# A hybrid attention layer: the first weight tiles are loaded directly behind the value slices, and the bias rows are read later

## The chip, the core and the metric

The kernel runs on one core of a Trainium2 chip. The metric is the device time of one execution in microseconds, the median of several runs. The core has five engines that run side by side and meet at semaphores: TensorE (matrix products, PE in the profile), ScalarE (ACT), VectorE (DVE), GpSimd (POOL) and SyncE (SP), which here issues nearly all transfers between the main memory and the on-chip memory.

## The reference, cut to what matters

```python
h = x @ W_in                                   # x: 256 x 1024, split into the parts below
ya = swa_sink_attention(qa, ka, va, sinks, table_a) * silu(za)   # window 128, 8 heads, 2 key heads
yb = moba_attention(qb, kb, vb, table_b) * silu(zb)              # 256 tokens: one causal block
merged = sigmoid(ga + b) * (ya @ w_out_a) + sigmoid(gb + b) * (yb @ w_out_b)
x = layer_norm(alpha * x + merged @ w_out, gamma, beta)
```

There are 256 tokens, 8 heads of width 64 in each of the two branches, and everything is float32. Both attentions add a learned bias to the scores that depends on the distance of query and key only.

## The kernel before, in words

**Products in three parts.** Each float32 matrix is split into a high part (a rounded copy) and a low part (what is left), and a product is high × high + low × high + high × low. In `contract` (L181, L182, L184) the two products with the high weights come first for all eight slices of the contraction, and then eight with the low weights. A weight tile therefore needs three steps before it is used up to its end: a load into a raw buffer (L133 on SP), a cast to the high part on ACT (L138), and a subtraction for the low part on DVE (L153).

**The stages.** First come the value projections: eight slices ("v", 0 to 7), each with its slice of x. Then 37 tiles ("t", n) of 512 KB, each one projection of 128 columns: t0 holds the keys of the first branch, t1 to t4 its queries, t5 to t12 keys and queries of the second branch in turn, t13 to t20 the inner gates, t21 to t36 the outer gates. The output weights ("a", "b", "o") follow.

**The order of the work is written out by hand.** Each engine executes its instructions in the order in which the program emits them. The list `order` (L93 to L105) says in which order things are fetched, with the bias rows ("r", n) placed between the tiles. `lead` (L167) is called just before a tile is used. It moves two cursors along `order`: the first calls `fetch` (the load, and the cast on ACT), the second calls `split` (the subtraction on DVE) and stays one item behind. How far ahead of the tile in use the cursors go is `far`, counted without the bias rows: 2 for the value slices, 2 for t0 to t2, 3 for t3 to t20, and so on. There are five raw buffers (`RAWS`), so a load has to wait for the split of the fifth item before it, and eight buffers each for high and low parts.

**What stands between.** `keys` (L192) and `queries` (L202) project a tile and take the result out of the accumulator with ACT and DVE: L196, L198 and a copy on POOL (L200) for the keys, L208 and L210 for the first queries (t1), L215, L216 and POOL copies (L220, L221) for the others. `scores` (L224) multiplies queries and keys, adds the bias rows `toep` (L235, L248), and takes the exponential on ACT (L250). `normalise` (L261) divides by the sums (L263 to L273), `turn` (L275) transposes on TensorE (L281).

The loop from L346 runs twelve steps. For the first steps it emits: step 0, the projection of t1; step 1, that of t2 and the first `scores`; step 2, `normalise` of those first scores, then the lead and the projection of t3, and the second `scores`; step 3, the projection of t4, the transposes of the first scores, and the third `scores`. At the head of each step stands `lead`, so that the casts and splits which it emits come ahead of the evictions of that step in the queues of ACT and DVE.

**The bias rows.** Each ("r", n) issues two transfers of 128 KB in pieces of 1 KB (L120). They read a small buffer in main memory that the kernel itself has written (L325), and the scores number n read them.

Of the kernel before, what the change touches and what calls it, by code (L numbers as in the profile page):

```python
# [35 lines left out]
KA, QA, KQB, ZA, ZB, GA, GB = 0, 1, 5, 13, 17, 21, 29  # L36
# [10 lines left out]
def hybrid_layer(ctx: ExitStack, tc: tile.TileContext, xT, x2, w_t, w_v, w_a, w_b, w_o,  # L47
# [43 lines left out]
    xh = const.tile([P, NK, S], F32R, name="xh")  # L91
    xl = const.tile([P, NK, S], F32R, name="xl")
    order = [("v", k) for k in range(NK)]  # L93
    for t in range(GA):
        order += [("t", t)]
        if QA <= t < KQB:
            order.append(("r", t - QA))
        elif KQB < t < ZA and (t - KQB) % 2:
            order.append(("r", 4 + (t - KQB) // 2))
    for g, w in ((GA, "a"), (GB, "b")):  # L100
        for c in range(8):
            order.append(("t", g + c))
# [3 lines left out]
    ahead = {"v": 2, "t": 3, "a": 4, "b": 5, "o": 7}  # L106
# [51 lines left out]
    def advance(stage, at, far):  # L158
        at += 1
        while at < len(order) and far:  # L160
            far -= order[at][0] != "r"
            at += 1
        while cursors[stage] < at:
            (fetch, split)[stage](*order[cursors[stage]])
            cursors[stage] += 1

    def lead(kind, n):  # L167
        at = order.index((kind, n))
        far = ahead[kind] if kind != "t" else 2 if n < 3 else 3 if n < GA else 4 if n < GB else 5
        advance(0, at, far)  # L170
        advance(1, at, far - 1)

    def weights(kind, n):
        lead(kind, n)
        return ready[kind, n]
# [170 lines left out]
    for i in range(12):  # L346
        if i == 2:
            normalise(*raised[0], True)
        lead("t", QA + i if i < 4 else KQB + 2 * (i - 4) if i < 8 else ZA + i - 8)
        if 3 <= i < 10:  # L350
            normalise(*raised[i - 2], i == 9)
        if 4 <= i < 8:
            keys(KQB + 2 * (i - 4), 1 + i % 2)
        if i < 8:
            queued[i] = queries(QA + i if i < 4 else KQB + 2 * (i - 4) + 1)
        else:
            acc = project(ZA + i - 8)
        if i >= 5 and i % 2:
            attend([(turned[n], 0 if n < 4 else P + (n - 4) * P) for n in (i - 5, i - 4)], ov[:, i - 5:i - 3, :])
        if 3 <= i < 11:  # L360
            turned[i - 3] = turn(raised[i - 3][0])
        if 1 <= i < 9:
            n = i - 1
            raised[n] = scores(queued[n], 0 if n < 4 else 1 + n % 2, 2 * n, 2 * n if n < 4 else None)
        if i >= 8:
            gate(i - 8, acc)
# [190 lines left out]
```

## Time and profile before

| | |
|---|---|
| median of three runs | 198.87 us (198.54 to 199.08) |
| the profiled execution | 198.86 us |
| its span on the core | 197.1 us |
| TensorE busy | 188.0 us (95%) |
| DVE, ACT, POOL busy | 136.7, 112.5, 44.1 us |
| moved by transfers | 37.43 MB, mean 190 GB/s |

The span is the time from the first to the last recorded instruction; the execution's own time holds some 1.8 us more. A row of the timeline gives the start in us, the duration in us, the engine, the line of the kernel, the operation, what it writes and reads, and in brackets the idle time of the engine before it with what ended it. Neighbouring instructions of one kind are merged ("x2").

### The profile page before, as it was taken

The page shows a single profiled execution, that of the slowest core. Times are in us where ns is not written, and L with a number is a line of the kernel's source. Part 1 is how long each engine was busy: PE and PEld are TensorE (multiplying, and loading weights), DVE is VectorE, ACT ScalarE, POOL GpSimd, SP SyncE. Part 2 cuts the span into 40 slices and gives each one's busy share as a digit, 9 for nine tenths or more (in the row PEclk, how much of TensorE's full clock was granted, in tenths as well). Part 3 has the DMA queues.
Part 4 walks back from the last instruction along what each step waited for, and adds up shares of the span by engine and source line. Part 5 has one row for each costly group of instructions (what it writes and reads, how often), then busy time and mean ns, then how long its engine had stood idle before and what let it go on. Part 6 is the DMA issues. An engine that isn't in the chain of part 4 may idle for free.

```text
span 197.1 us, 3919 instructions
## 1 busy us (share of the span) xinstructions
PE 188.0 (95%) x1469; PEld 178.0 (90%) x1469; DVE 136.7 (69%) x280; ACT 112.5 (57%) x223; POOL 44.1 (22%) x89
## 2 busy tenths in 40 slices
PE   8999999699999999999999999999999999999970
PEld 3799999599999999989999999999999999888860
DVE  0596277987897796686777547447585878696873
ACT  5575757479679669766679444246554746540110
POOL 7020043456599683100000000000000000004230
PEclk9999999999999999999999999999999999999996
DMA  5999999774363454044667865474847499400202
GB/s 139 306 400 346 266 288 318 193 249 149 120 195 126 122 147 166 7 150 170 209 209 234 299 221 152 170 224 145 288 145 266 139 323 334 170 0 0 104 3 106
DMA packets 14082, 37.43 MB, mean 190 GB/s; under 512 B 1632, under 2 KB 5744, under 8 KB 14064
## 3 DMA queue, kind: packets, MB, share of 16 engines
q1 hardware_dynamic: 13520, 36.51, 57.4%
q0 software_dynamic: 256, 0.49, 0.7%
q8 instruction: 11, 0.18, 0.4%
q10 hardware_dynamic: 288, 0.20, 0.3%
q14 instruction: 7, 0.06, 0.1%
HBM read 35.75 MB, written 1.44 MB: 189 GB/s over the span
## 4 chain that ended last, share of the span: by engine, by line
PE 77%; DMA 13%; DVE 4%; SPq 1%; issue 1%; ACT 1%; DVEq 0%; ACTq 0%
PE ps_acc L181 19%; PE ps_acc L182 19%; PE ps_acc L184 19%; PE ps_acc L424 6%; DMA wraw<-in_w_v 5%; DMA wraw<-in_w_t 5%; PE ps_sc L424 4%; DMA toep<-rd 4%; PE ps_pt L281 3%; PE ps_o L300 2%; DVE wl L153 2%; PE ps_sc L241 2%; PE ps_pt L424 1%; PE ps_sc L233 1%; PE ps_o L302 1%
## 5 line engine op out<-in xcount | busy, mean ns | idle before, releaser
L181 PE MATMUL ps_acc<-xh,wh 128*128 128x256 f32 x296 | 71.7, 281 | 0.0
L182 PE MATMUL ps_acc<-xl,wh 128*128 128x256 f32 x296 | 71.4, 280 | 0.0
L153 DVE TENSOR_TENSOR wl<-wraw,wh 128x1024 fp32r<-128x1024 f32 (+1 forms) x53 | 61.2, 1170 | 5.4 <-ACT wh L138 4.3
L138 ACT ACTIVATE wh<-wraw 128x1024 fp32r<-128x1024 f32 (+2 forms) x54 | 52.7, 989 | 8.4 <-DMA wraw<-in_w_t 5.0
L181 PEld LDWEIGHTS ps_acc<-xh,wh 128*128 128x128 f32 x296 | 55.8, 189 | 0.2 <-issue 0.2
L182 PEld LDWEIGHTS ps_acc<-xl,wh 128*128 128x128 f32 x296 | 55.8, 188 | 0.0
L184 PE MATMUL ps_acc<-xh,wl 128*128 128x256 f32 x296 | 41.0, 281 | 0.7 <-DVE wl L153 0.7
L184 PEld LDWEIGHTS ps_acc<-xh,wl 128*128 128x128 f32 x296 | 37.5, 188 | 0.9 <-DVE wl L153 0.9
L412 POOL CAST wh<-sums 128x2 fp32r<-128x2 f32 x8 | 1.5, 182 | 93.7 <-ACT sums L408 93.7
L379 ACT ACTIVATE sg<-ps_acc,bg 128x256 f32<-128x256 f32 x16 | 7.6, 475 | 19.3 <-PE ps_acc L184 19.2
L181 PE MATMUL ps_acc<-yh,wh 128*128 128x256 f32 x64 | 15.8, 281 | 0.0
L182 PE MATMUL ps_acc<-yl,wh 128*128 128x256 f32 x64 | 15.8, 280 | 0.0
L200 POOL CAST kall<-kall 64x512 fp32r<-64x512 f32 x10 | 10.7, 1065 | 14.9 <-DVE kall L198 14.3
L384 DVE TENSOR_TENSOR ga<-ps_acc,sg 128x256 f32<-128x256 f32 x8 | 3.4, 424 | 13.9 <-ACT wh L138 13.9
L181 PEld LDWEIGHTS ps_acc<-yh,wh 128*128 128x128 f32 x64 | 12.1, 188 | 0.0
L182 PEld LDWEIGHTS ps_acc<-yl,wh 128*128 128x128 f32 x64 | 12.0, 188 | 0.0
L389 ACT ACTIVATE mm<-m 128x256 fp32r<-128x256 f32 x8 | 3.4, 419 | 12.0 <-DVE m L388 12.0
L184 PE MATMUL ps_acc<-yh,wl 128*128 128x256 f32 x64 | 10.1, 279 | 0.0
L150 DVE TENSOR_TENSOR wl<-wraw,wh 128x1024 fp32r<-128x1024 f32 x8 | 9.7, 1218 | 0.1
L198 DVE TENSOR_TENSOR kall<-ps_acc,kall 64x256 fp32r<-64x256 f32 x10 | 4.2, 423 | 7.6 <-ACT kall L196 7.5
L424 PE MATMUL ps_acc<-wh,mm 128*128 128x512 f32 x32 | 8.8, 396 | 0.0
L184 PEld LDWEIGHTS ps_acc<-yh,wl 128*128 128x128 f32 x64 | 8.6, 188 | 0.0
(177 smaller groups left out, 302.6 us busy)
## 6 DMA issues: line engine op xcount, KB each, us to landing
wraw<-in_w_t SPq DMA_DIRECT2D x37, 512.0 KB, 3.9
wraw<-in_w_o SPq DMA_DIRECT2D x8, 512.0 KB, 5.0
wraw<-in_w_v SPq DMA_DIRECT2D x7, 320.0 KB, 5.3
toep<-rd SPq DMA_DIRECT2D x16, 128.0 KB, 7.0
wraw<-in_w_a SPq DMA_DIRECT2D x4, 512.0 KB, 3.3
wraw<-in_w_b SPq DMA_DIRECT2D x4, 512.0 KB, 4.5
xraw<-in_xT SPq DMA_DIRECT2D x8, 128.0 KB, 5.1
xr<-in_x SPq DMA_DIRECT2D x1, 1024.0 KB, 8.0
```

The source lines that it names most:

```text
L138: nc.scalar.activation(wh[:, cut], raw[:, cut], AF.Copy)
L150: nc.vector.tensor_sub(quarters(wl), raw.rearrange("p (a b) -> p a b", a=4), quarters(wh).bitcast(F32))
L153: nc.vector.tensor_sub(wl[:, :width], raw[:, :width], wh[:, :width].bitcast(F32))
L181: nc.tensor.matmul(acc, wh[:, cols[k]], ah[:, a0 + k, :], start=(k == 0), stop=False)
L182: nc.tensor.matmul(acc, wh[:, cols[k]], al[:, a0 + k, :], start=False, stop=False)
L184: nc.tensor.matmul(acc, wl[:, cols[k]], ah[:, a0 + k, :], start=False, stop=(k == n - 1))
L198: nc.vector.tensor_sub(l[r, j, :], acc[r, :], h[r, j, :].bitcast(F32))
L200: nc.gpsimd.tensor_copy(kall[halves[1 - j], b, :, j, :], kall[r, b, :, j, :])
L241: nc.tensor.matmul(o[:, j, :], q[:, j, P:], kall[:, b, part, j, :], start=(j == 0 and part == 0), stop=(j == 1 and part == 1))
L281: nc.tensor.transpose(pt[:, b * P:(b + 1) * P], pr[:, j, b * P:(b + 1) * P], ident)
L379: nc.scalar.activation(sg, acc, AF.Sigmoid, bias=bg[:, at:at + 1])
L424: nc.tensor.matmul(acc, a[:, k, ts], w[:, q:q + n, :cols], start=s0, stop=s1)
```

## The change

The bias rows leave their places behind t1, t2, t3, t4, t6, t8, t10, t12 and come behind t3 (two pairs), t4, t5, t7, t9, t11 and t13. `far` is 4 for all tiles up to t28 (it was 2 for t0 to t2 and 3 for t3 to t20). For the value slices, `far` grows at the end: `max(2, n - 3)` gives 3 for slice 6 and 4 for slice 7. In the order of emission this gives:

| at the lead of | fetched before | split before | fetched after | split after |
|---|---|---|---|---|
| v6 | t0 | v7 | t0 t1 | v7 t0 |
| v7 | t1 | t0 | t2 t3 | t1 t2 |
| t0 | r0 t2 | t1 | r0 r1 t4 | t3 |
| t1 | r1 t3 | t2 | r2 t5 | t4 |
| t2 | r2 t4 | t3 | r3 t6 | t5 |
| t3 | r3 t5 t6 | t4 t5 | t7 | t6 |
| t4 | r4 t7 | t6 | r4 t8 | t7 |
| t5 | t8 | t7 | t9 | t8 |

From there on everything is fetched and split one tile further ahead than before until t20, and from t22 on both orders are the same. No computation is added or removed.

```diff
     order = [("v", k) for k in range(NK)]
+
+    rows_at = {3: (0, 1), 4: (2,), 5: (3,), 7: (4,), 9: (5,), 11: (6,), 13: (7,)}
     for t in range(GA):
-        order += [("t", t)]
-        if QA <= t < KQB:
-            order.append(("r", t - QA))
-        elif KQB < t < ZA and (t - KQB) % 2:
-            order.append(("r", 4 + (t - KQB) // 2))
+        order += [("t", t)] + [("r", n) for n in rows_at.get(t, ())]
...
     def lead(kind, n):
         at = order.index((kind, n))
-        far = ahead[kind] if kind != "t" else 2 if n < 3 else 3 if n < GA else 4 if n < GB else 5
+        far = ahead[kind] if kind != "t" else 4 if n < GB else 5
+        if kind == "v":
+
+            far = max(far, n - 3)
         advance(0, at, far)
         advance(1, at, far - 1)
```

## The prediction

> **What bounds the kernel now.** I read the slices of the page first, then TensorE's own rows around the one bad slice, then what ACT, DVE and the loads did before it. Below, t0, t1, … are weight tiles in the order of use; r0, r1, … are pairs of bias rows, two transfers each; T4, T5, T6 are the times at which t4, t5, t6 have landed; "scores 0" is the first call of `scores`.
>
> ```profile
> PE   8999999699999999999999999999999999999970
> ```
>
> A slice is 4.93 us. TensorE is full from the second slice to the tail, except in the eighth (34.5 to 39.4 us). A tile that is ready earlier anywhere else buys nothing, and a delay that TensorE takes here is carried to the end, since no later slice has room.
>
> ```profile
> 29.15 0.40 PE L233 MATMUL ps_sc<-kall,q 128*128 128x256 f32 x2
> ...
> 29.87 0.28 PE L181 MATMUL ps_acc<-xh,wh 128*128 128x256 f32 x1
> ...
> 32.69 0.40 PE L233 MATMUL ps_sc<-kall,q 128*128 128x256 f32 x2
> ...
> 33.40 0.28 PE L181 MATMUL ps_acc<-xh,wh 128*128 128x256 f32 x1
> ...
> 35.17 0.28 PE L182 MATMUL ps_acc<-xl,wh 128*128 128x256 f32 x1
> 36.19 1.21 PE L184 MATMUL ps_acc<-xh,wl 128*128 128x256 f32 x8 [0.74 <-DVE wl L153]
> 37.23 0.82 PE L281 MATMUL ps_pt<-ident,pr__426 128*128 128x128 f32 x6
> 38.95 0.74 PE L233 MATMUL ps_sc<-kall,q 128*128 128x256 f32 x2 [0.90 <-DVE nm L248]
> ...
> 40.24 0.28 PE L181 MATMUL ps_acc<-xh,wh 128*128 128x256 f32 x1
> ```
>
> Scores 0 starts at 29.15 and takes 0.72; t3 takes 29.87 to 32.69 (2.82); scores 1 takes 0.71; t4 starts at 33.40. t4 then stops for the low part of its weights until 36.19, scores 2 waits until 38.95, and t5 starts at 40.24. The transposes in between take this long where nothing is waited for (chain of waits):
>
> ```profile
> 46.09 0.66 PE ps_pt L281 x6
> ```
>
> Without stops t5 would start at 33.40 + 2.82 + 0.66 + 0.71 = 37.6. The whole prize is 2.6 us. Who is late is seen on DVE:
>
> ```profile
> 27.76 0.88 DVE L210 SCALAR_TENSOR_TENSOR q<-ps_acc,q 64x256 fp32r<-64x256 f32 x2 [0.83 <-ACT q L208]
> 28.67 1.23 DVE L153 TENSOR_TENSOR wl<-wraw,wh 128x1024 fp32r<-128x1024 f32 x1
> 30.32 0.42 DVE L216 SCALAR_TENSOR_TENSOR ql<-ps_acc,qh 128x256 fp32r<-128x256 f32 x1 [0.42 <-ACT qh L215]
> ...
> 33.62 0.16 DVE L263 TENSOR_TENSOR sm<-sm,es 128x4 f32<-128x4 f32 x1 [0.75 <-ACT es L258]
> ...
> 34.03 0.97 DVE L270 TENSOR_SCALAR pr__426<-pr__426,rs 128x256 f32<-128x256 f32 x2
> 34.92 2.55 DVE L153 TENSOR_TENSOR wl<-wraw,wh 128x1024 fp32r<-128x1024 f32 x2
> 37.39 0.41 DVE L216 SCALAR_TENSOR_TENSOR ql<-ps_acc,qh 128x256 fp32r<-128x256 f32 x1
> ```
>
> This is one chain: L216 of t2 (30.32), the softmax of scores 0, its normalisation (33.62 to 35.0), the splits of t4 and t5 (2.55), L216 of t3 (37.39), and 2.85 later t5 on TensorE. The split of t4 stands behind the normalisation by program order alone, and so stops TensorE at 35.17.
>
> **The change part by part.** ACT's rows show its queue: each cast L138 of a tile stands where its load is issued, ahead of the evictions of that step.
>
> ```profile
> 17.30 1.06 ACT L138 ACTIVATE wh<-wraw 128x1024 fp32r<-128x1024 f32 x1 [0.62 <-DMA wraw<-in_w_t]
> 19.30 1.06 ACT L138 ACTIVATE wh<-wraw 128x1024 fp32r<-128x1024 f32 x1 [0.94 <-DMA wraw<-in_w_t]
> ...
> 22.93 1.06 ACT L138 ACTIVATE wh<-wraw 128x1024 fp32r<-128x1024 f32 x1 [1.10 <-DMA wraw<-in_w_t]
> 23.89 0.76 ACT L196 ACTIVATE kall<-ps_acc 64x256 fp32r<-64x256 f32 x2
> 25.86 1.07 ACT L138 ACTIVATE wh<-wraw 128x1024 fp32r<-128x1024 f32 x1 [1.22 <-DMA wraw<-in_w_t]
> 26.96 0.77 ACT L208 ACTIVATE q<-ps_acc 64x256 fp32r<-64x256 f32 x2
> 28.81 1.06 ACT L138 ACTIVATE wh<-wraw 128x1024 fp32r<-128x1024 f32 x1 [1.08 <-DMA wraw<-in_w_t]
> 29.90 0.39 ACT L215 ACTIVATE qh<-ps_acc 128x256 fp32r<-128x256 f32 x1
> ```
>
> The casts of t0 to t4 each wait for the load; t2, t3, t4 stand ahead of L196, L208, L215, the evictions of t0, t1, t2. With the change, `lead` asks for four tiles ahead where it asked for two, so the casts ahead of these three evictions are those of t4, t5 and t6. The splits on DVE move up with them: t4 ahead of L210, t5 ahead of L216 of t2, and only t6 behind the normalisation.
>
> *The split that leaves the chain.* Between normalisation and L216 of t3 stands one split of 1.23, not two of 2.55: 1.3 us gained. The stop of t4 at 35.17 goes with it.
>
> *The casts that come early.* Everything now hangs on T5 and T6. The chain of waits has the load of t6 (start, duration), and windows show the pace of the loads (time; last two columns: DMA share, GB/s):
>
> ```profile
> 24.11 8.92 DMA wraw<-in_w_t
> ```
> ```profile
> 14.00:17.00 3.00, 3.00 (x23) 3.00 (x22) 2.06 (x5) 1.79 (x3) 0.00 (x0) 1.00 1.03 414
> ...
> 20.00:23.00 3.00, 3.00 (x26) 3.00 (x25) 1.23 (x1) 1.86 (x6) 0.00 (x0) 1.00 1.06 270
> 23.00:26.00 3.00, 3.00 (x28) 3.00 (x27) 1.26 (x3) 1.77 (x4) 0.69 (x2) 1.00 1.06 267
> ...
> 48.50:49.50 1.00, 1.00 (x11) 1.00 (x10) 0.97 (x2) 0.44 (x2) 1.00 (x1) 1.00 0.85 267
> ```
>
> Before, t6 landed at 33.0. The loads are saturated: share over 1. At 414 GB/s, with no bias rows, a tile of 512 KB takes 1.27. A tile with a pair of rows takes 2.94 (22.93 to 25.86 to 28.81), which is the 267 to 270 GB/s of these windows. Rows alone, from the last window, take 0.84 a pair (256 KB at 267/0.85). So a mixture of rows and tiles costs some 0.8 more than both apart, a loss that the new order meets less often. From t0 at 17.3: t1, t2, t3 without rows at 1.27 each, 21.1; then r0, r1 and t4, 2.94 + 0.84 to 1.47 (half of 2.94), T4 = 24.9 to 25.5; r2 and t5, 2.94, T5 = 27.8 to 28.4; r3 and t6, 2.94, T6 = 30.8 to 31.4. But the bytes ahead of t6 are the same as before, t0 to t5 and four pairs, so if the loss goes by bytes, T6 stays 33.0 and T5 is r3's 0.84 to 1.5 ahead of where it was. I take T6 = 31.6, nearer to the grouped sum, and T5 = 28.6; the ends are 30.8 and 33.0. Issue does not hold this back:
>
> ```profile
> 13.44 0.82 DVE L153 TENSOR_TENSOR wl<-wraw,wh 128x640 fp32r<-128x640 f32 x1
> ...
> 15.17 0.83 DVE L153 TENSOR_TENSOR wl<-wraw,wh 128x640 fp32r<-128x640 f32 x1 [0.57 <-ACT wh L138]
> ```
> ```profile
> 14.32 1.26 SPq L120 DMA_DIRECT2D toep<-rd  x2
> 15.67 0.54 SPq L133 DMA_DIRECT2D wraw<-in_w_t  x1
> 16.26 1.16 SPq L120 DMA_DIRECT2D toep<-rd  x2
> 17.52 0.53 SPq L133 DMA_DIRECT2D wraw<-in_w_t  x1
> ```
>
> SP is passed in order, and five raw buffers mean that t2 needs the split of value slice 5 (ends 14.26) and t3 that of slice 6 (16.00). So t2's issue moves only from 15.67 to 14.3 and t3's from 17.52 to 16.0, still 5 us ahead of their landing; r0 and r1 (four issues of about 0.6) follow by 18.5.
>
> *TensorE at scores 0.* It needs the query of t1: cast of t5 (T5 + 1.06), then L208 to the end of L210, 26.96 to 28.64 = 1.68: T5 + 2.75 = 31.35, where it was 29.15, a stop of 2.2 us. The keys of t0 (L196 at T4 + 1.06, then copies on POOL) end earlier:
>
> ```profile
> 25.25 2.16 POOL L200 CAST kall<-kall 64x512 fp32r<-64x512 f32 x2 [14.18 <-DVE kall L198]
> ```
>
> From L196's start to that end is 3.52, so T4 + 4.6 = 29.9. From 31.35 TensorE alone would reach t5 after 0.72 + 2.82 + 0.71 + 2.82 + 0.66 + 0.71 = 8.44, at 39.8.
>
> *The chain on DVE.* Cast of t6 (T6 + 1.06), then L215 to L216 (0.42): L216 of t2 starts at 31.6 + 1.5 = 33.1, 2.8 later than 30.32. (The split of t5, T5 + 2.75 + 1.23 = 32.6, is done by then.) (I take ACT as passed in order, since its rows come in program order throughout.) From there to t5 on TensorE was 9.92; less one split, 8.6. t5 starts at 41.7, later than TensorE's own 39.8: DVE's chain ends last. 41.7 − 40.24 = **+1.5 us**. In general the change of time is T6 − 30.1.
>
> [...]
>
> *Priced at nothing.* The casts of t2 and t3 ahead of the value evictions: t3 cast by 22.2, the first bank free by 22.6, and t1 needs it at 23.47; were t3 landed only at 22.4, TensorE would stop some 0.4, inside the stop at scores 0. Rows read later: r0 lands by about 23 and scores 0 reads it after 31; r3 lands before t6. From r4 on the rows move by at most one tile, and with the loads past their crowd they have 5 us and more. One more tile ahead in t3 to t20 changes no wait, as TensorE has none after 40.24. If this cover were gone, each split that came late would cost its 1.23.
>
> Sum against the profiled execution: 198.86 (span 197.1 and 1.76 around it) + 1.5 = 200.4; the median shown is 198.87, the same.
>
> **The rivals.** *(B) Nothing gained in the loads:* mixed or not, t6 lands at 33.0. The same bytes speak for it, the windows against it. 33.0 − 30.1 = 2.9: 201.8. *(C) The loads run at their best:* all 6 tiles at 1.27 and 4 pairs at 0.84 from 17.3 put t6 at 28.3; the casts then wait for nothing that matters, L216 of t2 keeps its place, and the split that left the chain is pure gain: faster by 1.3, 197.6. It decides as soon as T6 is under 29.5 (0.6 faster). For it: t0 came at 414 GB/s. Against it: r2 and r3 still mix with t5 and t6. [...] *(D) Loss and gain cancel:* T6 between 29.5 and 30.7, within 0.3%: 198.9. *(E) The change does not do what it says,* because buffers hold the loads back: t2 and t3 are issued only 1.4 us earlier; if they land no earlier, it is B's time.
>
> **How the numbers follow.** 0.3% is 0.6 us, about what a measurement of this kernel can tell from no change. The forecast (T6 from 30.7 to 32.5) has 0.50; B with E (T6 beyond that) 0.18; C: 0.19; D: 0.13. Faster is C, 0.19; same is D, 0.13; slower is the rest, 0.68. The likeliest one's own range is 199.5 to 201.3. The range for all reaches down to C's nearer half, 198.2, and up to B and a little over, 202.0.
>
> **What would show it.** Right: TensorE stops 1.5 to 3.5 us at scores 0 with ACT standing in L138 of t5; L215 of t2 comes right behind the cast of t6; t4's eight L184 follow without a stop; one split between L270 and L216 of t3; bias rows never named as releaser. Wrong: t6 cast before 31, or L196 and L208 running ahead of a waiting cast, or t5 on TensorE before 40.2.

## The result, and the profile after

| | before | after |
|---|---|---|
| median of four runs | 198.77 us | 201.78 us (201.12 to 201.84) |
| ratio | | 1.0143, 95% interval 1.0117 to 1.0168 |
| the profiled execution | 198.86 us | 201.12 us |
| its span | 197.1 us | 199.3 us |

The change makes the kernel slower, by 2.8 us by the ratio and by 2.3 us in the two profiled executions. In the changed kernel most lines have moved: the cast is L136 (it was L138), the split L151 (L153), the eviction of the values L330 (L329), and the lines of `keys`, `queries` and `scores` are one further (L197, L209, L211, L217, L234, L242). The slices of TensorE and its rows, in the order of before:

```profile
PE   8799897989999999999999999999999999999970
```
```profile
21.14 0.31 PE L319 MATMUL ps_sc<-wl,xh 128*128 128x320 f32 x1
21.29 0.28 PE L182 MATMUL ps_acc<-xh,wh 128*128 128x256 f32 x1
...
24.92 0.39 PE L182 MATMUL ps_acc<-xh,wh 128*128 128x256 f32 x1 [0.64 <-ACT vv L330]
...
31.80 0.82 PE L234 MATMUL ps_sc<-kall,q 128*128 128x256 f32 x2 [0.96 <-DVE q L211]
...
41.22 0.74 PE L234 MATMUL ps_sc<-kall,q 128*128 128x256 f32 x2 [0.77 <-DVE nm L249]
41.94 0.74 PE L242 MATMUL ps_sc<-kall,q 128*128 128x256 f32 x4
42.52 0.28 PE L182 MATMUL ps_acc<-xh,wh 128*128 128x256 f32 x1
```

The stop of t4 is gone, and two new ones are there: at t1 (24.92, waiting for the eviction of the values) and at scores 0 (31.80). The one at scores 2 stays (0.77, before 0.90). t5 starts at 42.52 instead of 40.24, 2.3 us later, and nothing after it is late by more or less: from there to the end both take 156.8 us. Now ACT, whose queue is the cause:

```profile
17.44 1.06 ACT L136 ACTIVATE wh<-wraw 128x1024 fp32r<-128x1024 f32 x1 [0.63 <-DMA wraw<-in_w_t]
18.73 1.07 ACT L136 ACTIVATE wh<-wraw 128x1024 fp32r<-128x1024 f32 x1 [0.23 <-DMA wraw<-in_w_t]
20.00 1.06 ACT L136 ACTIVATE wh<-wraw 128x1024 fp32r<-128x1024 f32 x1 [0.20 <-DMA wraw<-in_w_t]
23.48 1.06 ACT L136 ACTIVATE wh<-wraw 128x1024 fp32r<-128x1024 f32 x1 [2.42 <-DMA wraw<-in_w_t]
24.45 0.75 ACT L330 ACTIVATE vv<-ps_acc 128x320 f32<-128x320 f32 x2
...
26.92 1.06 ACT L136 ACTIVATE wh<-wraw 128x1024 fp32r<-128x1024 f32 x1 [1.07 <-DMA wraw<-in_w_t]
27.89 0.75 ACT L197 ACTIVATE kall<-ps_acc 64x256 fp32r<-64x256 f32 x2
29.34 1.07 ACT L136 ACTIVATE wh<-wraw 128x1024 fp32r<-128x1024 f32 x1 [0.71 <-DMA wraw<-in_w_t]
30.44 0.77 ACT L209 ACTIVATE q<-ps_acc 64x256 fp32r<-64x256 f32 x2
32.20 1.06 ACT L136 ACTIVATE wh<-wraw 128x1024 fp32r<-128x1024 f32 x1 [0.99 <-DVE q L211]
33.28 0.38 ACT L216 ACTIVATE qh<-ps_acc 128x256 fp32r<-128x256 f32 x1
```

These are the casts of t0 to t6 and the evictions between them. The value products ended at 21.45, but their eviction began at 24.45, behind the cast of t3, which had waited 2.42 us for its load. That ACT is passed in order the prediction took from the order of its rows; here it is measured on an eviction that was ready: held for 3.0 us, 2.0 of them while the cast in front of it waited for its load. The cast of t6 is put down to DVE, but its load, in the chain of waits, ended just before:

```profile
25.34 6.78 DMA wraw<-in_w_t
```

So t6 landed at 32.1, only 0.9 earlier than before. DVE's chain follows from it, with one split behind the normalisation instead of two:

```profile
33.70 0.42 DVE L217 SCALAR_TENSOR_TENSOR ql<-ps_acc,qh 128x256 fp32r<-128x256 f32 x1 [0.33 <-ACT qh L216]
...
37.44 0.97 DVE L271 TENSOR_SCALAR pr__440<-pr__440,rs 128x256 f32<-128x256 f32 x2
38.33 1.41 DVE L151 TENSOR_TENSOR wl<-wraw,wh 128x1024 fp32r<-128x1024 f32 x1
39.67 0.41 DVE L217 SCALAR_TENSOR_TENSOR ql<-ps_acc,qh 128x256 fp32r<-128x256 f32 x1
```

The pace of the loads, in the windows of before (the last column is GB/s):

```profile
17.00:20.00 3.00, 3.00 (x23) 3.00 (x22) 2.07 (x3) 2.13 (x3) 0.00 (x0) 1.00 1.03 401
20.00:23.00 3.00, 3.00 (x25) 3.00 (x25) 2.27 (x2) 1.06 (x1) 0.00 (x0) 1.00 1.07 251
23.00:26.00 3.00, 2.36 (x20) 2.16 (x20) 1.23 (x1) 2.37 (x5) 0.00 (x0) 1.00 1.05 292
26.00:29.00 3.00, 3.00 (x28) 3.00 (x27) 0.33 (x1) 1.70 (x3) 0.00 (x0) 1.00 1.02 307
```

Nearly without rows, to 20 us, the loads run at 401 GB/s (before: 294 in that window) and t1 and t2 land 1.3 apart. From 20 us, with the rows r0 and r1 and t3 under way together, they run at 251. SP's own row for the issue of t5 shows something that I had not looked for:

```profile
23.44 0.33 SPq L131 DMA_DIRECT2D wraw<-in_w_t  x1
```

SP had stood 2.2 us before this issue, until t3 landed at 23.4. t5 and t6 were asked for earlier than before, but issued at 23.44 and 25.34, where it had been 23.51 and 24.11. The last section comes back to this.

### The profile page after: what moved, and what is told of

Read it like the earlier page. It is cut to its first block, busy times and chain, and to the rows that moved or that the text cites. A ratio compares the mean times of both kernels' runs of the same rounds, so it can differ in the third digit from the quotient of the medians.

```text
span 199.3 us, 3920 instructions
## 1 busy us (share of the span) xinstructions
PE 188.8 (95%) x1469; PEld 178.0 (89%) x1469; DVE 136.9 (69%) x280; ACT 112.7 (57%) x223; POOL 43.8 (22%) x89
## 4 chain that ended last, share of the span: by engine, by line
PE 76%; DMA 12%; DVE 5%; ACT 3%; issue 1%; SPq 1%; DVEq 0%; POOL 0%; ACTq 0%
PE ps_acc L182 19%; PE ps_acc L185 19%; PE ps_acc L183 19%; DMA wraw<-in_w_t 7%; PE ps_acc L425 6%; DMA wraw<-in_w_v 5%; PE ps_sc L425 4%; PE ps_pt L282 3%; PE ps_o L301 2%; PE ps_sc L242 2%; PE ps_pt L425 1%; ACT wh L136 1%; DVE wl L151 1%; PE ps_sc L234 1%; PE ps_o L303 1%
## 5 line engine op out<-in xcount | busy, mean ns | idle before, releaser
L151 DVE TENSOR_TENSOR wl<-wraw,wh 128x1024 fp32r<-128x1024 f32 (+1 forms) x53 | 61.3, 1169 | 7.9 <-ACT wh L136 7.5
L136 ACT ACTIVATE wh<-wraw 128x1024 fp32r<-128x1024 f32 (+2 forms) x54 | 52.9, 989 | 10.5 <-DMA wraw<-in_w_t 5.3
L185 PE MATMUL ps_acc<-yh,wl 128*128 128x256 f32 x64 | 10.1, 279 | 0.0
```

The costliest lines, as they stand in the source:

```text
L136: nc.scalar.activation(wh[:, cut], raw[:, cut], AF.Copy)
L151: nc.vector.tensor_sub(wl[:, :width], raw[:, :width], wh[:, :width].bitcast(F32))
L185: nc.tensor.matmul(acc, wl[:, cols[k]], ah[:, a0 + k, :], start=False, stop=(k == n - 1))
```

## The experiments

Two questions: is it the cast ahead of the evictions, and its load, that costs, or something else in the change; and why did the loads gain so little? A table of all runs comes last.

**Each part of the change alone.** First the lookahead, with the rows where they were:

```diff
-        far = ahead[kind] if kind != "t" else 2 if n < 3 else 3 if n < GA else 4 if n < GB else 5
+        far = ahead[kind] if kind != "t" else 4 if n < GB else 5
+        if kind == "v":
+            far = max(far, n - 3)
```

> Only the lookahead of the change, with the bias rows at their places of before. Theory (casts of t4, t5, t6 hold the evictions of t0, t1, t2 on ACT until the tiles have landed; change of time = landing of t6 minus 30.1): rows and tiles alternate as before, t6 lands at about 33.0, so +2.9 us, 201.7. Rival (it is the later bias rows that cost): no change, 198.9.

Measured: 203.0 us, ratio 1.0212 (1.0163 to 1.0261), 4.2 us slower and 1.3 more than my theory gave. Then the rows alone, with the line `far` of before:

> Only the later places of the bias rows, with the lookahead of before. Theory: the casts ahead of the three evictions are those of t2, t3, t4, which land no later than before, so nothing is lost, and the two splits stay behind the normalisation, so nothing is gained: 198.6 to 199.2. Rival (the later rows cost): 201 or more, with a wait for the rows or for a tile that they delay.

Measured: 198.5, ratio 0.9993 (0.9965 to 1.0022). So all of the loss comes with the lookahead, and the later rows take some of it away. In its profiled execution the lookahead alone costs 3.4 us (202.29 against 198.86). Why the lookahead alone cost more shows in the waits of TensorE and in rows of ACT and DVE:

```profile
PE ps_acc L184 <- ACT vv L332: 3.4, 1, 3.4
```
```profile
25.50 1.06 ACT L138 ACTIVATE wh<-wraw 128x1024 fp32r<-128x1024 f32 x1 [1.89 <-DMA wraw<-in_w_t]
26.47 0.75 ACT L332 ACTIVATE vv<-ps_acc 128x320 f32<-128x320 f32 x2
...
30.75 1.06 ACT L138 ACTIVATE wh<-wraw 128x1024 fp32r<-128x1024 f32 x1 [0.59 <-DMA wraw<-in_w_t]
```
```profile
32.64 0.88 DVE L213 SCALAR_TENSOR_TENSOR q<-ps_acc,q 64x256 fp32r<-64x256 f32 x2 [0.19 <-ACT q L211]
33.54 1.23 DVE L153 TENSOR_TENSOR wl<-wraw,wh 128x1024 fp32r<-128x1024 f32 x1
34.80 0.42 DVE L219 SCALAR_TENSOR_TENSOR ql<-ps_acc,qh 128x256 fp32r<-128x256 f32 x1
```

Here t3 landed at 25.4, the values were evicted behind its cast, and TensorE stood 3.4 us at t1 for want of a free accumulator. I had priced that wait at nothing. Still, the chain that ended last does not run over this stop. It runs over t5: landed at 30.7 and cast from 30.75, it held the eviction of t1 on ACT, then L213 and the split of t5 stood on DVE in front of L219 of t2, which started at 34.80, 4.5 later than before (L216, 30.32). Less the one split of 1.3 that left the chain, that is 3.2 of the 3.4. T6 (32.7) alone would have given 2.6. The eviction L218 on ACT, which did wait for TensorE, ended at 34.58, 0.2 before the split of t5: the stop at t1 was nearly as late, but did not set the time. Where the rest of the 4.2, outside the profiled execution, lies no trace shows. A second effect follows the stop, told in the last section.

**The rows left out.** If the landing is what counts, the changed order must win once the loads are quick.

```diff
-            for a in (2 * n, 2 * n + 1):
-                ...
-                nc.sync.dma_start(toep[:, a, :], src)
             return
...
+            nc.gpsimd.memset(toep, 0.0)
```

> The changed kernel without the loads of the bias rows (the bias is left out, its tile is zero). Theory: t1 to t6 land 1.27 us apart, t6 at about 25, before its cast is due; no eviction is held, L216 of t2 comes 0.6 earlier than before and the normalisation is followed by one split: 197.0, faster than the kernel before. Rival (the order of casts and splits costs by itself, whatever the loads do): 201 to 201.8 as with the rows.

> The kernel before without the loads of the bias rows (the bias is left out, its tile is zero). It is the control for the changed kernel without rows, 197.7. Theory: before, the loads do not set the end, the two splits behind the normalisation do; L215 of t2 no longer waits for the cast of t4, 0.6 earlier at most: 198.1 to 198.8. Rival (leaving the rows out makes any order faster by about 1): 197.7 or less.

Measured: the changed kernel without rows 197.7, ratio 0.9951 (0.9925 to 0.9978); the kernel before without rows 198.8, ratio 1.0007 (0.9971 to 1.0044). The same order of casts and splits that loses 2.8 us with the rows gains 1.0 without them, and leaving the rows out does nothing to the kernel before. The rival that the order costs by itself has fallen. The gain is 0.7 short of the 197.0 expected. ACT and DVE in the changed kernel without rows:

```profile
27.62 1.06 ACT L132 ACTIVATE wh<-wraw 128x1024 fp32r<-128x1024 f32 x1
29.34 0.39 ACT L212 ACTIVATE qh<-ps_acc 128x256 fp32r<-128x256 f32 x1 [0.65 <-PE ps_acc L181]
```
```profile
28.93 1.23 DVE L147 TENSOR_TENSOR wl<-wraw,wh 128x1024 fp32r<-128x1024 f32 x1
30.19 0.42 DVE L213 SCALAR_TENSOR_TENSOR ql<-ps_acc,qh 128x256 fp32r<-128x256 f32 x1
```

The cast of t6 waits for nothing, and ACT is in time for t2; now the split of t5 stands in front of that query on DVE and keeps it at 30.19, where I had put it at 29.7 (0.6 ahead of before).

**The casts at their old place, the loads at the new one.** `fetch` is cut in two, a load and a cast with a cursor of its own; loads go four ahead, casts and splits as before.

```diff
+        near = ahead[kind] if kind != "t" else 2 if n < 3 else 3 if n < GA else 4 if n < GB else 5
         advance(0, at, far)
-        advance(1, at, far - 1)
+        advance(1, at, near)
+        advance(2, at, near - 1)
```

> The loads and rows in the order of the change, but casts and splits at the lookahead of before (two for t0 to t2, three from t3). Theory: the casts ahead of the three evictions are those of t2, t3, t4 again, which have landed by 27; no stop at scores 0; two splits behind the normalisation: 198.3 to 198.9. Rival (the order of the loads costs, by t3 landing at 23.4 or by SP held): 201 to 201.8.

Measured: 198.6, ratio 0.998 (0.9951 to 1.001). Issuing the loads early costs nothing and gains nothing; what cost was the place of the casts and splits. The next kernels move the splits alone forward again. Here the two splits are together on DVE's chain, as before:

```profile
34.65 2.54 DVE L158 TENSOR_TENSOR wl<-wraw,wh 128x1024 fp32r<-128x1024 f32 x2
```

**The split off the chain, without the early casts.** In the kernel with the rows alone, in the last kernel and in the kernel before, one line is changed so that the splits go two tiles ahead from the start (in the last kernel it is the line of the third cursor):

```diff
-        advance(1, at, far - 1)
+        advance(1, at, 2 if kind == "t" and n < GA else far - 1)
```

> Later bias rows and the lookahead of before for loads and casts; only the splits of t0 to t2 go two tiles ahead instead of one, so that t4 is split ahead of L216 of t2 and t5 alone behind the normalisation. Theory (one split off the chain is worth 1.3, and t4 has landed and been cast by 28.5): no stop at t4, t5 on TensorE 1.3 earlier, 197.2. Rival (the split off the chain is worth nothing, the stop at scores 2 has another cause): 198.5 as with the rows alone.

> Loads and rows in the order of the change, casts at the lookahead of before, splits of t0 to t2 two tiles ahead. Theory: as the kernel with later rows and early splits, 197.2, since the earlier loads are waited for by nothing. Rival (the earlier loads help or hurt by themselves): differs from it by over 0.6.

> The kernel before with the splits of t0 to t2 two tiles ahead and nothing else; the rows stay at their places. Theory: t4 lands at 28.8 and is cast by 29.9, so its split ends at 31.1 and puts L216 of t2 0.8 later; one split less on the chain gives 1.3 back: 0.5 faster, 198.3, against 1.7 with the rows moved. Rival (the place of the rows has no part in the gain): 197.1 as with the rows moved.

Measured: with the rows moved 197.1, ratio 0.991 (0.9881 to 0.994), the lowest median of all, ahead of both kernels; with the loads early as well 197.5, ratio 0.9924 (0.9888 to 0.996), the same; and in the kernel before, rows unmoved, 198.2, ratio 0.9958 (0.9931 to 0.9985). All three lie within 0.3 us of what was expected. The splits of t4 and t5 around L214 of t2 and t3, with the rows moved:

```profile
29.01 1.23 DVE L151 TENSOR_TENSOR wl<-wraw,wh 128x1024 fp32r<-128x1024 f32 x1 [0.41 <-ACT wh L136]
30.27 0.42 DVE L214 SCALAR_TENSOR_TENSOR ql<-ps_acc,qh 128x256 fp32r<-128x256 f32 x1
...
34.87 1.21 DVE L151 TENSOR_TENSOR wl<-wraw,wh 128x1024 fp32r<-128x1024 f32 x1
36.01 0.41 DVE L214 SCALAR_TENSOR_TENSOR ql<-ps_acc,qh 128x256 fp32r<-128x256 f32 x1
```

and with the rows at their old places:

```profile
30.32 1.23 DVE L153 TENSOR_TENSOR wl<-wraw,wh 128x1024 fp32r<-128x1024 f32 x1 [0.84 <-ACT wh L138]
31.58 0.43 DVE L216 SCALAR_TENSOR_TENSOR ql<-ps_acc,qh 128x256 fp32r<-128x256 f32 x1
```

The later rows, worth nothing alone, are worth 1.3 here in the profiled executions and about 1.0 by the ratios: they bring t4 in before its split is due, so the query of t2 is done (L214) from 30.27 and not (L216) from 31.58. The next step, in the kernel with the loads early as well, is no split at all behind the first normalisation:

```diff
-        advance(2, at, 2 if kind == "t" and n < GA else near - 1)
+        advance(2, at, 1 if (kind, n) == ("t", 3) else 2 if kind == "t" and n < GA else near - 1)
```

> As the last, with the split of t5 moved from behind the first normalisation to the next step, so that no split stands between it and L216 of t3. Theory: scores 2 waits no more, t5 starts at 37.6 to 38, 196.3 to 196.8; but two splits now stand ahead of the second normalisation, and if scores 3 has no room for one of them, up to 1.2 come back: 197.5.

Measured: 197.3, ratio 0.9925 (0.9901 to 0.9948), no better. t5 starts at 38.56 and not at 38.96, but from there to the end it takes 0.4 us longer: what the first chain gave came back behind it, as the expectation had allowed. On DVE the query of t3 now waits for ACT, where it stands behind the casts of t5 and t6.

```profile
35.70 0.42 DVE L226 SCALAR_TENSOR_TENSOR ql<-ps_acc,qh 128x256 fp32r<-128x256 f32 x1 [0.78 <-ACT qh L225]
```

**The change with rows placed still later.** Nothing left out, the whole lookahead kept:

```diff
-    rows_at = {3: (0, 1), 4: (2,), 5: (3,), 7: (4,), 9: (5,), 11: (6,), 13: (7,)}
+    rows_at = {5: (0, 1), 6: (2,), 7: (3,), 8: (4,), 9: (5,), 11: (6,), 13: (7,)}
```

> The changed kernel with its whole lookahead, only the first bias rows placed still later: r0, r1 behind t5, r2 behind t6, r3 behind t7, r4 behind t8. Nothing is left out. Theory (the change of time is the landing of t6 minus 30.1, and not under -1.3): t1 to t5 land without rows between, t5 at 23.7, t6 with r0 and r1 at 27.5 to 28.5, before its cast is due: 197.5 to 197.9, faster than the kernel before although every load, cast and split is ordered as far ahead as in the change. Rival (the deeper lookahead or the number of rows cost, wherever the rows stand): 201 and more; or the rows come too late for scores 0: a wait of L235's line for them.

Measured: 198.7, ratio 0.9971 (0.9946 to 0.9996). The loss of 2.8 us is gone, the rival fell, but the gain I expected did not come. The cast of t6 and the start of t5 on TensorE:

```profile
30.13 1.06 ACT L136 ACTIVATE wh<-wraw 128x1024 fp32r<-128x1024 f32 x1 [1.95 <-DMA wraw<-in_w_t]
```
```profile
40.48 0.28 PE L182 MATMUL ps_acc<-xh,wh 128*128 128x256 f32 x1
```
```profile
20.00:23.00 3.00, 3.00 (x26) 3.00 (x25) 1.80 (x2) 1.72 (x2) 0.00 (x0) 1.00 0.97 334
23.00:26.00 3.00, 3.00 (x26) 2.91 (x25) 1.64 (x2) 2.99 (x8) 0.00 (x0) 1.00 1.03 235
```

T6 came at 30.1 and not at 28; by the rule "T6 minus 30.1" that is no change, and t5 starts 0.2 later than before. So the rule holds and my reckoning of the loads does not: r0 and r1, beside t5 and t6, again pulled the rate down, to 235 GB/s, and t5 landed at 26.0 and not at 23.7.

**Why the mixture is slow.** The rows' pieces of 1 KB start 4 bytes apart, eight pieces over nearly the same bytes. Two kernels read as many pieces elsewhere:

```diff
-                src = bass.AP(tensor=rd.tensor, offset=..., ap=[[RW + 8, 16], [1, 8], [1, S]])
+                src = xT[:, a % 8, :]                      # one kernel
+                src = bass.AP(tensor=rd.tensor, offset=..., ap=[[RW, 16], [RL, 8], [1, S]])   # the other
```

> The changed kernel, but each bias row transfer reads as many 1 KB pieces from the input x (128 pieces, 8 KB apart) instead of the small buffer of the bias, so the bias is replaced by other numbers; order, sizes and issues are the same. Theory (the loss where rows and tiles mix comes from the way the rows read the bias buffer): as in the value stage, where 1 KB pieces of x and value slices ran at 399 GB/s together, the mixture keeps 380 to 410 GB/s; t3 lands at 21.1, t6 by 28.5, time 197.5 to 198. Rival (any 1 KB pieces beside 4 KB pieces are slow): t6 at 32, 201 to 202.

> The changed kernel, but the 128 pieces of a row transfer are read from 128 separate places of the bias buffer, 1536 bytes apart, instead of from 16 places with eight pieces each, 4 bytes apart; the bias is replaced by wrong bias values. If the loss comes from pieces that overlap or start off a boundary: 197.5 to 198, t6 by 28.5. If it comes from the buffer itself (small, just written): t6 at 32, 201 to 202.

Measured: rows read from x 199.2, ratio 1.0017 (0.9991 to 1.0043); rows read from separate places of the bias buffer 198.6, ratio 0.9985 (0.9957 to 1.0013). By the ratios both are 2.5 to 3.1 us faster than the change; t3 landed at 21.8 and 22.2, not at 23.4; and in the window where the change ran at 251 GB/s they ran at 374 and 376; here the second of them:

```profile
20.00:23.00 3.00, 3.00 (x26) 3.00 (x25) 1.81 (x2) 1.75 (x2) 0.00 (x0) 1.00 1.05 376
```

So it is neither the 1 KB pieces nor the buffer, but how the pieces lie in it; whether the overlap or the odd starts do it was not separated. Both fell short of 198: t6 was cast at 29.33 and 30.01, not by 28.5. At these rates its load should have come sooner. The share of busy transfer engines falls under 1 in places (0.91 from 23 to 26 us with x), and SP again issued t5 only when t3 had landed (21.76 and 21.82 with x, 22.20 and 22.27 with separate places), so issue on SP may hold it; no run separates this.

| kernel | median us | ratio | cast of t6 starts | t5 on TensorE |
|---|---|---|---|---|
| before | 198.8 | 1 | 34.4 | 40.24 |
| the change | 201.8 | 1.0143 | 32.20 | 42.52 |
| lookahead only | 203.0 | 1.0212 | 32.75 | 43.63 |
| rows at later places only | 198.5 | 0.9993 | | |
| change, late casts | 198.6 | 0.998 | | |
| change, rows after t5 | 198.7 | 0.9971 | 30.13 | 40.48 |
| change, rows read from separate places | 198.6 | 0.9985 | 30.01 | 40.31 |
| change, rows read from x | 199.2 | 1.0017 | 29.33 | 39.66 |
| change, no rows | 197.7 | 0.9951 | 27.62 | 38.86 |
| before, no rows | 198.8 | 1.0007 | | |
| rows later, early splits | **197.1** | 0.991 | | 38.85 |
| change, late casts, early splits | 197.5 | 0.9924 | | |
| the same, split of t5 later | 197.3 | 0.9925 | | |
| before, early splits | 198.2 | 0.9958 | | |

In the four kernels with the early cast in which that cast waited for its load (32.20, 30.13, 30.01, 29.33), t5 follows it by 10.32, 10.35, 10.30 and 10.33 us. With rows from separate places the profile puts this wait down to DVE, but t6 landed at 29.93, just before. With rows from x the split of t5 on DVE ended together with ACT's eviction of t2, at 30.8, so there both set the pace.

## Why the prediction was right, and where it was off

**The direction and the mechanism were right.** The forecast was slower by 1.5; measured 2.8 by the ratio and 2.3 between the profiled executions. The casts of t4, t5 and t6 stand before the evictions of t0, t1 and t2, ACT waits in them for loads, and with the loads left early, moving casts and splits back gives the time of before (198.6), and the splits forward again 197.5: what costs is the place of the casts. (The splits of the change go one tile further than in that kernel; no run moves the casts alone.)

**The gain was sized right.** One split off the chain at 1.3: in the traces of the three kernels with early splits t5 starts 1.4, 1.3 and 0.1 earlier than before (38.85, 38.96, 40.17), as the landing of t4 let it, and by the ratios they got 1.8, 1.5 and 0.8. The split itself grew to 1.41 in the change.

**The term that was mis-sized is T6.** I took 31.6, between 30.8 (loads grouped) and 33.0 (rival B, nothing gained); it came at 32.1, 0.5 later. The grouped sum failed at its first group. t1 and t2 landed as worked out (18.6 and 19.9 against casts at 18.73 and 20.00), but t3 at 23.4 and not 21.1. I had counted the loss of the mixture behind t3, with t4; it fell on t3 itself, because the rows are issued as soon as t3 is and run beside it. From T6 on the sum nearly held: 10.4 from the landing of t6 to t5 where it had 10.1. That the median, 201.8, is the very figure of B and lies above the 199.5 to 201.3 of the likeliest case is chance: t6 did not land at 33.0. The 2.8 are 2.0 by T6, 0.3 by the rest of the chain and 0.5 to 0.6 that the profiled execution does not have.

**"Issue does not hold this back" was wrong.** The sum had t2's and t3's issue right (14.46 and 15.60), but t5 was held until t3 had landed, and t6 was issued 1.2 later than before. The transfer engines were busy all the while (share 1.02 to 1.07), so no run shows whether this made T6 later.

**The stops of TensorE were there, smaller and elsewhere.** At scores 0 it stopped 0.96, not 2.2 and not the 1.5 to 3.5 that I had named as a sign, because 0.64 had gone at t1 and because t0's products began at 21.29 and not at 20.64, behind a stop of 1.0 at 6.35 us that kernels with other orders show too. I had priced the stop at t1 at 0.4 if t3 landed only at 22.4, and inside the one at scores 0; in the change it costs nothing of its own, since DVE's chain ends last. With the lookahead alone another term was wrong: the split of t5, T5 + 2.75 + 1.23, which I took to be done in time. That needs t6 to land 2.5 or more after t5. In the change it was 2.9, with the lookahead alone 2.0, and there the split ended last.

**The rivals.** C, loads at their best, would have been 197.6: without rows the changed kernel is at 197.7. D, no change, would need T6 near 30: with the rows after t5 T6 is 30.1 and the time is the one of before within 0.3%. E, loads held back by buffers, fell: t1 and t2 landed 1.3 apart, and t5 waited with its buffer free. The other executions of the change took 0.7 more than the profiled one (201.8 against 201.12), and the median of the kernel with rows from x is 0.9 above its profiled one; where that time lies no trace shows.

## What to carry to other kernels

ACT's rows came in program order here, so a conversion of prefetched data was a wait for its load, placed in front of everything that came after it (3.0 us for the eviction of the values in the change; with the loads as early and the casts at their old place the time was 198.6). So the load may be issued early, but put the conversion behind the evictions of the step, and count its place by the time of landing and not by the number of tiles. A lookahead that helps on one engine's chain (here one split on DVE) may be had without the one that hurts on another (here the casts on ACT), by giving each its own cursor. And a transfer moved out of the way may be worth nothing until something can use the time it frees: the later rows gave 0 alone and about 1 us together with the earlier splits.

## What the runs showed of the hardware that I had not expected

**Half the clock after a stop of 3.35 us.** In the profiled execution of the kernel with the lookahead only, TensorE stood for 3.35 us at t1. Then its matmuls came 0.21 us apart and not 0.12, at a granted clock of 0.50 (windows; the third column from the right is the granted clock):

```profile
25.00:26.00 1.00, 0.00 (x0) 0.00 (x0) 0.00 (x0) 0.50 (x1) 0.00 (x0) 1.00 1.04 287
26.00:27.00 1.00, 0.06 (x1) 0.06 (x1) 0.41 (x1) 1.00 (x3) 0.00 (x0) 0.73 1.10 242
27.00:28.00 1.00, 1.00 (x5) 1.00 (x6) 0.82 (x1) 0.87 (x3) 0.00 (x0) 0.50 1.03 275
28.00:29.00 1.00, 1.00 (x6) 1.00 (x6) 0.00 (x0) 0.56 (x1) 0.00 (x0) 0.50 1.04 312
29.00:30.00 1.00, 1.00 (x7) 1.00 (x6) 0.00 (x0) 0.99 (x3) 0.00 (x0) 0.56 1.01 390
```

The sixteen matmuls from 26.94 took 3.30 us until 30.24; at 0.12 each they would take 1.9, so the clock cost TensorE about 1.4, an estimate from these two. It is no term of that kernel's 4.2, since the chain over t5 ended later still. By the windows the half clock lasted from about 26.5 to 29.9, 3.4 us, and began 2.9 us after TensorE's last matmul before the stop. The stops of 0.64 and 0.96 us in the change left the clock at 1.00. How long a stop has to be, and what ends the half clock, no run shows.

**How the rows' pieces lie in memory changed the rate of what ran beside them.** With eight overlapping pieces at 4 bytes' distance, loads and rows together moved 251 GB/s from 20 to 23 us, and t3 landed at 23.4; with as many pieces 1536 bytes apart in the same buffer it was 376, and t3 landed at 22.2. Over the 3 us of that window this is 0.38 MB less. What in the overlapping pieces takes the time, no run shows.

**Eight transfers of SP at a time.** In the traces of the kernel before and of the change SP issued none of its 93 transfers before the eighth one ahead of it in its order had landed; the shortest time from that landing to the issue is 0.02 us in both. The seventh ahead was still under way at 16 issues before and at 19 in the change. In the change t5 stands eight behind t3, with four rows, t4 and two more rows between, and its issue followed the landing of t3 by 0.06 us (23.38, 23.44). So this load, asked for early behind many small transfers, was not issued early. Whether the chip or the program's own bookkeeping sets the eight, no run shows.
